# Value products with differences of two blocks' values, the sink column written a block ahead, and an attention layer whose order a model of the run decides

## The chip, the cores and the metric

The kernel runs on one core of a Trainium2 chip. The metric is the device time of one launch in microseconds (us), as the median of several runs.

## The reference, cut to what matters

Two residual layers, each behind an RMSNorm, then a last RMSNorm. The first is grouped-query attention with a sliding window and one learned sink for each head, the second a pooling mixer. S = 4096 tokens, D = 1024, 16 query heads over 4 key/value heads of 64, float32 throughout.

```python
def swa_with_sinks(q, k, v, sinks):            # blocks of 128 tokens
    kc, vc = band(k), band(v)                  # the block before and the block itself
    s = einsum('bnqhgd,bnkhd->bnhgqk', qb, kc) * (1.0 / sqrt(HEAD_DIM))
    diff = qi + BLOCK - kj
    in_band = (diff >= 0) & (diff < WINDOW)    # WINDOW = 128
    s = where(in_band & not_pad, s, -inf)
    m = maximum(max(s, axis=-1), sink)
    p = exp(s - m)
    p = p / (p.sum(-1) + exp(sink - m))
    return einsum('bnhgqk,bnkhd->bnqhgd', p, vc)

def attn_layer(h, w_in, sinks, w_out):
    q, k, v, z = split(h @ w_in)
    return (swa_with_sinks(q, k, v, sinks) * silu(z)) @ w_out

def pool_layer(h, w_in, w_mix, scale, w_out):
    u, z = split(h @ w_in)
    p = multiscale_pool(u)                     # windows 2, 4, 8, 16, one for each group
    m = einsum('bsgc,gcd->bsgd', p, w_mix).reshape(B, S, 1024) * scale
    return (m * silu(z)) @ w_out
```

## The kernel before

**Numbers.** TensorE multiplies in a rounded float32 (`fp32r`). Each operand is therefore split into a high half (a copy by ScalarE, ACT) and a low half (source minus high half, by VectorE, DVE), and each product is made three times: high by high, high by low, low by high (`split_sb`, L129; `PASSES`). Such a copy into `fp32r` is called CAST in the profile.

**Steps and units.** The attention layer goes through the tokens in 8 steps `s` of 512. A step consists of units of 256 output columns: `k`, four `q`, `v`, four `z` (the gate) and, for the step before, four `out`. A unit is 48 matmuls of 128x512 (L267), the `v` unit 96 of 128x256 (L277); step 0 has 10 units and the others 14. Unit weights arrive in two halves of 1 MB. In step 0 `w_load` fetches them, `w_split` splits them and writes the halves to DRAM (`wparts`). Later steps fetch them back by `w_again` (L156), into three buffers. All DMAs named here are issued on SyncE's queue (SP).

**Attention blocks.** Between the units' matmuls lie the 16 blocks of a step, one for each key head `j` and each 128 queries `b`; `2_2_3` means step 2, `j` 2, `b` 3, and "block 10" counts them from 0. Each block is two tiles of 64 queries, which see 192 keys. A block has three parts. `it_scores` (L368): ACT writes the negated sink beside the scores into the PSUM tile `s`, of which there is one buffer (L370); PE makes eight matmuls 128x192 (L375); DVE folds the first and the last 64 keys into the same 64 columns, since a query uses just one of each pair (L380), and takes the extreme (L384); ACT makes four exponentials with their sums (L387); DVE takes the reciprocal and GpSimd (POOL) multiplies (L390). `it_turn` (L393): PE transposes `P` into `pT`, a PSUM tile of two buffers shared with `po`; ACT copies it to the high half of `m1` (L404); DVE makes the low half (L405) and, in other rows, a part of `m2` (L410). In the folded rows a probability belongs either to the earlier or to the later key. POOL's `affine_select` therefore keeps in `m1` the later keys alone (`upto`, L417), and in `m2` the earlier keys alone (`after`, L414 and L419). `it_pv` (L422): six value products into `po`, for each tile two of `m1` with the block's own values (`vm` or `vn`, L432) and one of `m2` with the earlier values (`vp` or `vq`, L433); ACT and DVE bring the result into `o`.

**Values.** `ev_v` (L318) splits the `v` unit's result into the two half-partition parts of `vm`. `v_twice` sends them by DMA to the other 64 partitions of `vp` and `vq`, and `v_again` copies to `vn` on POOL and to `vp`, `vq` on ACT.

**The next layer's weights.** From step 2 on, `seven_load` and `seven` (L510) split the pooling layer's weights, and write them to DRAM, four pieces a step. Each piece becomes four or seven casts on ACT (`part_u`, `part_z`, `part_o`, L130), whose tiles take turns in two `sl` slots: a cast can start when the DMA of the cast two before it has landed. The weight of `u` is first multiplied with `w_mix` in step 0 (`prep_load`, `prep_mm`).

**What sets the order.** Nothing is in a written order. `at(t, fn, ...)` gives each piece a time in units, and the table `T` (L35) holds the offsets: `turn` units after a block's scores come its transposes, `pv` later its products. At the end the pieces are issued in order of time:

```python
for t, _, fn, args in sorted(events, key=lambda e: e[:2]):
    fn(*args)
```

The builder then orders each engine's queue with a list scheduler: it steps through a modelled run and takes the earliest issued instruction that is ready by its model. So the queues follow `T` only roughly, and any change in one engine's work can move instructions on the others.

Of the kernel before, what the change touches and what calls it, by code (L numbers as in the profile page):

```python
# [8 lines left out]
F32 = mybir.dt.float32  # L9
# [11 lines left out]
G = 512  # L21
# [5 lines left out]
NKV = 4  # L27
# [7 lines left out]
T = dict(sqA=2.5, sqAd=0.82, rsA=5.5, sqB=5.8, sqBd=0.5, rsB=7.95, tot=0.8, spr=0.3, xs=2.3, frs=5.3, fin=6.8, turn=0.9, pv=0.8, ws0=1.0, ws1=0.3, wr0=1.0, wr1=0.5, vt=0.25, vtd=0.5, k0=2.9, kd0=0.8, k1=6.1, kd1=0.8, k2=9.3, kd2=0.8, k3=12.5, kd3=0.8, wl0=2.0, wl1=1.2, res=1.55, xl=1.5, hc=0.01, a0=2.3, a1=4.6, a2=6.8, a3=9.3, ad=0.55, op=0.5, e0=2.9, e1=5.14, e2=7.38, e3=9.62, ed=0.56, pl=1.3, pm=0.5, pmd=0.5, aturn=0.9, apv=0.8, kt=0.2)  # L35
# [10 lines left out]
def f32(ap):  # L46
    return ap.bitcast(F32)
# [3 lines left out]
def trunk_kernel(ctx, tc, xt, xm, ng, w_a_in, sinks, w_a_out, wu_t, wmix, pscale, w_b_z, w_b_out, fg, out):  # L51
# [55 lines left out]

    vm = sp.tile([128, NB + 1, NKV, 128], F32R, tag="vm", name="vm")
    vn = sp.tile([128, NB, NKV, 128], F32R, tag="vn", name="vn")
    vp = sp.tile([128, NB + 1, NKV, 128], F32R, tag="vp", name="vp")  # L110
    vq = sp.tile([128, NB + 1, NKV, 128], F32R, tag="vq", name="vq")
    nc.vector.memset(kt[:, :, :, 0:128].bitcast(F32), 0.0)
    nc.vector.memset(vm[64:128, 0].bitcast(F32), 0.0)
    nc.vector.memset(vp[:, 0].bitcast(F32), 0.0)
    nc.vector.memset(vq[:, 0].bitcast(F32), 0.0)
# [202 lines left out]
    def ev_v(U, s):  # L318
        ps = acc.pop(U)
        if s > 0:  # L320
            for t in (vm[64:128], vp, vq):
                nc.gpsimd.tensor_scalar(t[:, 0], f32(t[:, NB]), 1.0, 1.0, op0=ALU.mult, op1=ALU.mult)
        ps = ps.rearrange("p a (b d) -> p (a b) d", d=64)
        for r in (0, 1):
            src = ps[64 * r:64 * r + 64]
            own = vm[64 * r:64 * r + 64, r:r + NB]
            v = own.rearrange("p b j d -> p (b j) d")
            nc.scalar.copy(v[:, :, 0:64], src)
            nc.vector.tensor_sub(v[:, :, 64:128], src, f32(v[:, :, 0:64]))

    def v_twice():
        upper, lower = f32(vm[0:64, 0:NB]), f32(vm[64:128, 1:NB + 1])
        nc.sync.dma_start(f32(vp[64:128, 1:]), upper)
        nc.sync.dma_start(f32(vq[0:64, 1:]), lower)

    def v_again(b):
        for r, before in ((0, vp), (1, vq)):
            rows = slice(64 * r, 64 * r + 64)
            src = f32(vm[rows, b + r])
            nc.gpsimd.tensor_scalar(vn[rows, b], src, 1.0, 1.0, op0=ALU.mult, op1=ALU.mult)  # L340
            nc.scalar.copy(before[rows, b + 1], src)
# [26 lines left out]
    def it_scores(s, j, b):  # L368
        ps = rpsum.tile([128, 4, 256], F32, tag="s", bufs=1, name=f"s{s}_{j}_{b}")
        nc.scalar.copy(view(ps, 1, [(512, 2), (447, 2)]), nsink[:, j].unsqueeze(2).to_broadcast([128, 2, 2]))  # L370
        for c in range(2):
# [13 lines left out]
        P = sp.tile([128, 4, 136], F32, tag="P", bufs=2, name=f"P{s}_{j}_{b}")  # L385
        for i in range(4):
            nc.scalar.activation(P[:, i, 0:129], view(ps, 1 + 512 * (i // 2) + 319 * (i % 2), [(1, 129)]), AF.Exp,  # L387
                                 bias=mx[:, i:i + 1], scale=-1.0, accum_out=sm[:, i:i + 1])
        nc.vector.reciprocal(sm, sm)  # L389
# [3 lines left out]
    def it_turn(s, j, b):  # L393
# [6 lines left out]

        m1 = sp.tile([128, 2, 4, 128], F32R, tag="m1", bufs=1, name=f"m1_{s}_{j}_{b}")
# [5 lines left out]
        mu = m1.rearrange("p l (c u) x -> p u l c x", c=2)  # L407
        for u in range(2):
            wr, other = slice(64 * u, 64 * u + 64), slice(64 - 64 * u, 128 - 64 * u)
            nc.vector.tensor_sub(m2[other, u], pu[wr, u], f32(mu[wr, u, 0]))  # L410
            after = dict(pattern=[[0, 4], [-1, 64]], base=-1, channel_multiplier=1)
            upto = dict(pattern=[[0, 4], [0, 2], [1, 64]], base=0, channel_multiplier=-1)
            src = f32(mu[wr, u, 0]).rearrange("p c (r q) -> p c r q", r=2)
            nc.gpsimd.affine_select(out=m2[wr, u].rearrange("p c (r q) -> p c r q", r=2), in_=src, compare_op=ALU.is_ge, fill=0.0,  # L414
                                    **{**after, "pattern": [[0, 2], [0, 2], [-1, 64]]})
            mv = mu[wr, u].rearrange("p l c (r q) -> p (l c) r q", r=2)
            nc.gpsimd.affine_select(out=mv, in_=f32(mv), compare_op=ALU.is_ge, fill=0.0, **upto)  # L417
            mv = m2[other, u].rearrange("p c (r q) -> p (c r) q", r=2)
            nc.gpsimd.affine_select(out=mv, in_=f32(mv), compare_op=ALU.is_ge, fill=0.0, **after)  # L419
        its[s, j, b] = (m1, m2)  # L420

    def it_pv(s, j, b):  # L422
        m1, m2 = its.pop((s, j, b))
        if b == 0:
            obufs[s, j] = sp.tile([128, 2, G], F32, tag="o", bufs=2, name=f"o{s}_{j}")
# [37 lines left out]
    def prep_load(g):  # L463
# [5 lines left out]
        split_sb(pw[g][:, 0], pw[g][:, 1], raw)  # L469
        for c in range(2):  # L470
# [3 lines left out]
            split_sb(t[:, 0], t[:, 1], raw)  # L474
# [360 lines left out]
    def unit(kind, s, j, t):  # L835
# [12 lines left out]
        elif s == 0:  # L848
# [3 lines left out]
            at(t - T["ws1"], w_split, u, 1, key)  # L852
# [40 lines left out]
    for g in range(1, 4):  # L893
        at(g - T["pl"], prep_load, g)
        for hf in range(2):
            at(g - T["pm"] + T["pmd"] * hf - 0.0005, prep_mm, g, hf)
# [237 lines left out]
```

## Time and profile before

| | us |
|---|---|
| median of 3 runs | 2742.24 |
| lowest and highest run | 2738.83, 2743.64 |
| the profiled execution's own time | 2741.26 |
| its span, first to last instruction | 2739.2 |
| attention layer, steps 0 to 7, about | 0 to 1700 |

A row of the profile's groups reads: line, engine, operation, output and inputs by the program's names (numbers left out; a name can stand for several tiles, `m` for `m1` and `m2`), shape and type, count; behind the first bar busy us and mean ns of one; behind the second the engine's idle time just before them and what released it. PE is TensorE's matmuls, PEld its weight loads. A row of the waits reads: what waited, for whom, us in total, times, longest. "x (n)" in a row of stretches is busy time and instructions. The granted clock is TensorE's, as a share of its full rate.

### The profile page before, as it was taken

Reading aid. Unit: us, or ns where it says so; the run is one execution under the profiler, and the core shown is the slowest. Engines: PE = TensorE matmul, PEld = TensorE weight load, DVE = VectorE, ACT = ScalarE, POOL = GpSimd, SP = SyncE. Lnnn points to the kernel's source line nnn. Section 1 sums busy time; section 2 is a strip of 40 time slices with the busy share of each in tenths; the row PEclk is TensorE's granted clock in tenths of the full one; section 3 lists DMA queues with packets and bytes.
Section 4 is the critical chain, followed back from the end, with each engine's and each line's share of the span. In section 5 each row is a group of like instructions: output and inputs, shape, how many; then the busy total and the mean of one; then the engine's idle time right before and its main releaser. Section 6 shows DMA issues by size and latency. Waiting matters only on the chain.

```text
span 2739.2 us, 35678 instructions
## 1 busy us (share of the span) xinstructions
PE 2602.2 (95%) x12604; PEld 2159.3 (79%) x12604; DVE 1626.7 (59%) x2546; ACT 1066.1 (39%) x2728; POOL 701.1 (26%) x1122
## 2 busy tenths in 40 slices
PE   7889998999998998999998999999999999999998
PEld 6778877877877886887887887788878887887786
DVE  6667666457456557556557556747455755655544
ACT  4556444445445445345444443313312331322121
POOL 0345443434334345335345333000000000000000
PEclk9999998999999999999999999999999999999999
DMA  7856766667667668667667555657577758757752
GB/s 285 278 200 226 264 215 221 226 223 251 230 211 272 231 200 250 232 215 267 225 200 257 191 200 210 237 192 263 175 242 256 263 195 288 267 186 244 255 200 100
DMA packets 175197, 626.10 MB, mean 229 GB/s; under 512 B 23198, under 2 KB 33438, under 8 KB 145324
## 3 DMA queue, kind: packets, MB, share of 16 engines
q1 hardware_dynamic: 175020, 623.83, 67.5%
q8 instruction: 100, 1.64, 0.2%
q14 instruction: 77, 0.63, 0.1%
HBM read 489.47 MB, written 117.51 MB: 222 GB/s over the span
## 4 chain that ended last, share of the span: by engine, by line
PE 50%; DVE 15%; DMA 14%; issue 13%; ACT 7%; POOL 1%; SPq 1%; ACTq 0%; POOLq 0%; DVEq 0%
PE mm L267 23%; DMA fin<-x 3%; PE mm L277 3%; PE s L375 2%; DMA out<-fin 2%; ACT P L387 2%; DMA w<-wparts 2%; DMA w_u<-part_u 2%; PE po L432 1%; DVE q L315 1%; PE pT L398 1%; DMA xm<-in_xm 1%; PE X_3u L620 1%; PE X_3z L620 1%; DVE m L410 1%
## 5 line engine op out<-in xcount | busy, mean ns | idle before, releaser
L267 PE MATMUL mm<-h,w 128*128 128x512 f32 x3456 | 871.2, 405 | 0.0
L267 PEld LDWEIGHTS mm<-h,w 128*128 128x128 f32 x3456 | 652.8, 194 | 140.9
L267 PE MATMUL mm<-a,w 128*128 128x512 f32 x1536 | 365.8, 393 | 4.2 <-DMA w<-wparts 2.4
L267 PEld LDWEIGHTS mm<-a,w 128*128 128x128 f32 x1536 | 284.2, 188 | 63.0 <-DMA w<-wparts 2.9
L390 POOL TENSOR_TENSOR P<-P,sm 128x516 f32<-128x516 f32 x128 | 135.5, 1059 | 463.4 <-DVE sm L389 459.1
L387 ACT ACTIVATE P<-s,mx 128x129 f32<-128x129 f32 x512 | 182.2, 370 | 140.9 <-DVE mx L384 138.2
L417 POOL TENSOR_SCALAR_AFFINE_SELECT m<-m 64x512 fp32r<-64x512 f32 x256 | 184.6, 721 | 54.3 <-DVE m L410 49.9
L747 POOL TENSOR_TENSOR rs<-ms,mhalf 128x4 f32<-128x4 f32 x7 | 7.0, 1007 | 742.1 <-DVE ms L746 742.1
L375 PEld LDWEIGHTS s<-kt,q 128*128 128x128 f32 x1024 | 135.2, 196 | 66.3 <-ACT s L370 52.1
L375 PE MATMUL s<-kt,q 128*128 128x192 f32 x1024 | 142.5, 281 | 43.2 <-ACT s L370 33.9
L414 POOL TENSOR_SCALAR_AFFINE_SELECT m<-m 64x256 fp32r<-64x256 f32 x256 | 109.9, 429 | 254.7 <-ACT m L404 246.0
L439 ACT COPY tmp<-po 64x256 f32<-64x256 f32 x256 | 94.1, 367 | 125.2 <-PE po L433 87.3
L440 DVE TENSOR_TENSOR o<-po,tmp 64x256 f32<-64x256 f32 x256 | 107.8, 421 | 45.9 <-ACT tmp L439 40.9
L315 DVE SCALAR_TENSOR_TENSOR q<-mm,q 64x512 fp32r<-64x512 f32 x128 | 88.1, 689 | 73.9 <-ACT q L314 72.6
L314 ACT ACTIVATE q<-mm 64x512 fp32r<-64x512 f32 x128 | 76.0, 593 | 138.0 <-DVE q L315 83.0
L419 POOL TENSOR_SCALAR_AFFINE_SELECT m<-m 64x256 fp32r<-64x256 f32 x256 | 123.5, 482 | 16.7
L410 DVE TENSOR_TENSOR m<-pT,m 64x256 fp32r<-64x256 f32 x256 | 108.2, 422 | 7.9
L405 DVE TENSOR_TENSOR m<-pT,m 128x512 fp32r<-128x512 f32 x128 | 88.0, 687 | 39.9 <-ACT m L404 38.9
L277 PE MATMUL mm<-w,h 128*128 128x256 f32 x768 | 100.6, 290 | 10.7 <-DMA w<-wparts 10.7
L277 PEld LDWEIGHTS mm<-w,h 128*128 128x128 f32 x768 | 97.9, 197 | 12.6 <-DMA w<-wparts 11.9
L380 DVE COPY_PREDICATED s<-mask,s 128x256 f32<-128x256 int8 x128 | 54.4, 425 | 89.8 <-PE s L375 79.0
L387 ACT ACTIVATION_READ_ACCUMULATOR P<-s,mx 128x1 f32 x512 | 104.5, 204 | 0.0
(356 smaller groups left out, 4545.5 us busy)
## 6 DMA issues: line engine op xcount, KB each, us to landing
w<-wparts SPq DMA_DIRECT2D x196, 1024.0 KB, 6.0
wparts<-w SPq DMA_DIRECT2D x28, 1024.0 KB, 4.8
xt<-in_xt SPq DMA_DIRECT2D x32, 512.0 KB, 4.5
res<-in_xt SPq DMA_DIRECT2D x32, 512.0 KB, 5.2
x<-res SPq DMA_DIRECT2D x32, 512.0 KB, 5.7
xr<-x SPq DMA_DIRECT2D x32, 512.0 KB, 6.1
xm<-in_xm SPq DMA_DIRECT2D x28, 512.0 KB, 6.0
w_u<-part_u SPq DMA_DIRECT2D x56, 256.0 KB, 3.5
```

Source lines behind the costliest of these rows:

```text
L267: nc.tensor.matmul(ps[:, c], w[:, wl, k % 4, 128 * c:128 * c + 128], rhs(k, hl), start=(k == 0 and i == 0), stop=(k == NK - 1 and i == 2))
L277: nc.tensor.matmul(ps[:, b], hts[s, k][:, hl, 128 * b:128 * b + 128], wtiles[U, k // 4][:, wl, k % 4], start=(k == 0 and i == 0), stop=(k ...
L315: nc.vector.scalar_tensor_tensor(dst[64 - r:128 - r], src, -SCALE, f32(dst[r:r + 64]), op0=ALU.mult, op1=ALU.subtract)
L375: nc.tensor.matmul(ps[:, 2 * c + u, 2 - 2 * u:194 - 2 * u], qs[s, j][:, c, 2 * b + u].rearrange("p r x -> p (r x)"), kt[:, j, hl, t:t + 19 ...
L387: nc.scalar.activation(P[:, i, 0:129], view(ps, 1 + 512 * (i // 2) + 319 * (i % 2), [(1, 129)]), AF.Exp, bias=mx[:, i:i + 1], scale=-1.0, ...
L390: nc.gpsimd.tensor_mul(P[:, :, 0:129], P[:, :, 0:129], sm.unsqueeze(2).to_broadcast([128, 4, 129]))
L410: nc.vector.tensor_sub(m2[other, u], pu[wr, u], f32(mu[wr, u, 0]))
L414: nc.gpsimd.affine_select(out=m2[wr, u].rearrange("p c (r q) -> p c r q", r=2), in_=src, compare_op=ALU.is_ge, fill=0.0, **{**after, "patt ...
L417: nc.gpsimd.affine_select(out=mv, in_=f32(mv), compare_op=ALU.is_ge, fill=0.0, **upto)
L419: nc.gpsimd.affine_select(out=mv, in_=f32(mv), compare_op=ALU.is_ge, fill=0.0, **after)
L439: nc.scalar.copy(tmp[d:d + 64], pv[e:e + 64, r])
L440: nc.vector.tensor_add(dst, pv[d:d + 64, r], tmp[d:d + 64])
```

## The change

**Values.** `ev_v` now keeps the whole result in float32 (`vf`, 128x1024), splits the block's own values for all 128 partitions (`vn`), then forms earlier values minus own values in PSUM, and splits these differences into `vp` (lower half of the partitions) and `vq` (upper half). `v_twice` sends those to the other halves, and `v_again` copies `vn` to `vm` on POOL alone. The products of `m1`, no longer masked, with the own values then count the folded rows as if all belonged to the later key, and those of `m2`, masked to the earlier keys, with the difference correct it. So the select `upto` is gone, 256 instructions on POOL; the matmuls are as many and of the same shapes.

**Sink.** The sink column of the following block is written right behind a block's exponentials (`s_open`, `opened`, `following`).

**Step 0.** The low half of every unit's second weight half, but for `out`, and of six of `prep_load`'s twelve pieces goes to POOL. The last two of the four `prep_load` come earlier.

**Spacing.** In `T`, the transposes and products follow the scores after .72 and .55 units instead of .9 and .8 (steps 1 to 6), the first product of a step comes no earlier than 4.5 units into it, and step 1 has its own order of units.

**Order.** All pieces of the attention layer's eight steps are issued in one block of the program, whose queues the builder orders by a finer model of the run's times; the rest follows as before.

```diff
     def ev_v(U, s):
...
+        src = ps.rearrange("p b (j d) -> p (b j) d", d=64)
+        nc.scalar.copy(vf[:, 1:], ps)
+        nc.scalar.copy(v[:, :, 0:64], src)
+        nc.vector.tensor_sub(v[:, :, 64:128], src, f32(v[:, :, 0:64]))
+        nc.vector.tensor_sub(ps, vf[:, 0:NB], ps)
+        for r, t in ((0, vp), (1, vq)):
+            rows = slice(64 * r, 64 * r + 64)
+            v = t.rearrange("p b j d -> p (b j) d")[rows]
+            nc.scalar.copy(v[:, :, 0:64], src[rows])
+            nc.vector.tensor_sub(v[:, :, 64:128], src[rows], f32(v[:, :, 0:64]))
...
         for i in range(4):
             nc.scalar.activation(P[:, i, 0:129], ...)
+        if (s, j, b) in following:
+            opened[following[s, j, b]] = s_open(*following[s, j, b])
...
-            mv = mu[wr, u].rearrange("p l c (r q) -> p (l c) r q", r=2)
-            nc.gpsimd.affine_select(out=mv, in_=f32(mv), compare_op=ALU.is_ge, fill=0.0, **upto)
...
             at(t - T["ws0"], w_split, u, 0, key)
-            at(t - T["ws1"], w_split, u, 1, key)
+            at(t - T["ws1"], w_split, u, 1, key, None if kind == "out" else nc.gpsimd)
...
-                at(t + turn + pv, it_pv, s, j, b)
+                at(max(t + turn + pv, base + T["pv0"]), it_pv, s, j, b)
...
-    for t, _, fn, args in sorted(events, key=lambda e: e[:2]):
+    early = [e for e in events if e[0] < base - A_OUT]
+    with tc.block(schedule_with_timeline_sim=True):
+        for _, _, fn, args in early:
+            fn(*args)
+    for _, _, fn, args in events[len(early):]:
         fn(*args)
```

How the queues move is shown at three places. A row is a line of the code, an operation, its output and inputs with their running numbers, the shape, and how often it stands there in a row.

ACT in step 2, from the exponentials (`P`) of block 2_2_2 to those of block 2_2_3, before: `m1` is the copy of the transposes, `tmp` that of the products, `s` the sink, `part_o` the casts.

```order
L387 ACTIVATE P2_2_2_5434,sm2_2_2_5432<-s2_2_2_5420,mx2_2_2_5431 128x129 x4
L439 COPY tmp2_2_0_5458<-po2_2_0_5451 64x256
L404 CAST m1_2_2_1_5477<-pT2_2_1_5472 128x512
L370 COPY s2_2_3_5556<-nsink_146 128x2x2
L130 CAST part_o0_0_1_6141<-raw7_o0_0_6060 128x256
L130 CAST part_o0_0_2_6145<-raw7_o0_0_6060 128x256
L130 CAST part_o0_0_3_6149<-raw7_o0_0_6060 128x256
L130 CAST part_o0_1_0_6567<-raw7_o0_1_6448 128x256
L387 ACTIVATE P2_2_3_5570,sm2_2_3_5568<-s2_2_3_5556,mx2_2_3_5567 128x129 x4
```

The same stretch after:

```order
L395 ACTIVATE P2_2_2_5367,sm2_2_2_5365<-s2_2_2_5270,mx2_2_2_5364 128x129 x4
L374 COPY s2_2_3_5372<-nsink_146 128x2x2
L445 COPY tmp2_2_0_5315<-po2_2_0_5308 64x256
L131 CAST part_o0_0_0_6030<-raw7_o0_0_5955 128x256
L315 ACTIVATE q2_3_5376<-mm34_5225 64x8x64
L131 CAST part_o0_0_1_6034<-raw7_o0_0_5955 128x256
L131 CAST part_o0_0_2_6038<-raw7_o0_0_5955 128x256
L445 COPY tmp2_2_1_5421<-po2_2_1_5414 64x256 x2
L415 CAST m1_2_2_2_5472<-pT2_2_2_5467 128x512
L131 CAST part_o0_0_3_6042<-raw7_o0_0_5955 128x256
L131 CAST part_o0_1_0_6451<-raw7_o0_1_6342 128x256
L395 ACTIVATE P2_2_3_5500,sm2_2_3_5498<-s2_2_3_5372,mx2_2_3_5497 128x129 x4
```

The sink has moved ahead of the copies, and the four casts in a row have become one and two pairs with other work between them.

PE in the same step, from the transposes (`pT`) of block 2_2_2 to its products (`po`), before; `mm` are the units' matmuls.

```order
L398 MATMUL pT2_2_2_5596<-ident_140,P2_2_2_5434 128x128 x4
L267 MATMUL mm35_5463<-h2_7_3972,w35_1_5396 128x512 x6
L267 MATMUL mm36_5626<-h2_0_3780,w36_0_5470 128x512 x6
L267 MATMUL mm36_5626<-h2_1_3791,w36_0_5470 128x512 x6
L267 MATMUL mm36_5626<-h2_2_3821,w36_0_5470 128x512 x6
L267 MATMUL mm36_5626<-h2_3_3867,w36_0_5470 128x512 x6
L267 MATMUL mm36_5626<-h2_4_3877,w36_1_5548 128x512 x6
L375 MATMUL s2_3_0_5666<-kt_160,q2_3_5441 128x192 x8
L432 MATMUL po2_2_2_5687<-m1_2_2_2_5601,vm_161 128x2x128 x2
L433 MATMUL po2_2_2_5687<-m2_2_2_2_5602,vp_163 128x2x128
L432 MATMUL po2_2_2_5687<-m1_2_2_2_5601,vn_162 128x2x128 x2
L433 MATMUL po2_2_2_5687<-m2_2_2_2_5602,vq_164 128x2x128
```

After:

```order
L408 MATMUL pT2_2_2_5467<-ident_140,P2_2_2_5367 128x128 x4
L383 MATMUL s2_2_3_5372<-kt_160,q2_2_4945 128x192 x6
L268 MATMUL mm35_5385<-h2_6_3902,w35_1_5303 128x512 x6
L268 MATMUL mm35_5385<-h2_7_3906,w35_1_5303 128x512 x6
L268 MATMUL mm36_5529<-h2_0_3734,w36_0_5392 128x512 x6
L268 MATMUL mm36_5529<-h2_1_3781,w36_0_5392 128x512 x6
L438 MATMUL po2_2_2_5549<-m1_2_2_2_5472,vm_161 128x2x128 x2
L268 MATMUL mm36_5529<-h2_2_3790,w36_0_5392 128x512 x2
L439 MATMUL po2_2_2_5549<-m2_2_2_2_5473,vp_163 128x2x128
L438 MATMUL po2_2_2_5549<-m1_2_2_2_5472,vn_162 128x2x128 x2
L439 MATMUL po2_2_2_5549<-m2_2_2_2_5473,vq_164 128x2x128
```

Twenty-four of the units' matmuls now stand between the transposes and the first products, where 36 stood.

SP at the start of step 3, before: `w40` is the weight of its `v` unit, `kt` the copy of the keys to the other partitions.

```order
L174 DMA xt4_0_7349<-in_xt 128x1024
L158 DMA w40_0_6054<-wparts_2_0_507 128x2048
L238 DMA rsq_4_116<-rs_4_6660 128x4
L304 DMA kt_160<-kt_160 64x2x512 x4
L158 DMA w40_1_6094<-wparts_2_1_593 128x2048
L242 DMA bc4_6664<-rsq_4_116 128x512
L174 DMA xt4_1_7426<-in_xt 128x1024
```

After, to the first weight of the unit behind it:

```order
L180 DMA xm4_3_6259<-in_xm 128x1024
L175 DMA xt4_0_7232<-in_xt 128x1024
L159 DMA w40_1_5997<-wparts_2_1_622 128x2048
L305 DMA kt_160<-kt_160 64x2x512 x4
L175 DMA xt4_1_7294<-in_xt 128x1024
L239 DMA rsq_4_116<-rs_4_6542 128x4
L159 DMA w41_0_6074<-wparts_14_0_2426 128x2048
```

The second half of the `v` unit's weight now stands ahead of the four copies of `kt`.

80 lines of the change are left out of this document (40 added, 40 removed).

## The prediction

> **What bounds the kernel now.** I read the page first, then the waits of TensorE (PE), then busy time in stretches cut at the same place of every step, then the timeline of ScalarE (ACT) where PE waits.
>
> ```profile
> span 2739.2 us, 35678 instructions
> PE 2602.2 (95%) x12604; PEld 2159.3 (79%) x12604; DVE 1626.7 (59%) x2546; ACT 1066.1 (39%) x2728; POOL 701.1 (26%) x1122
> ```
>
> PE is the bound, and the change leaves its matmuls as many and as large as they were. So only PE's idle time and its clock can give something. Stretches (length; busy time of PE, weight loads, DVE, ACT and POOL; granted clock; DMA share; GB/s): first the front of a step, then the tails, blocks 10 to 15, of steps 1 to 6.
>
> ```profile
> 262.00:382.00 120.00, 118.60 (x606) 99.57 (x604) 74.07 (x125) 60.63 (x175) 53.19 (x82) 1.00 0.73 250
> 382.00:478.00 96.00, 82.95 (x406) 69.86 (x407) 60.66 (x101) 41.55 (x114) 43.34 (x62) 0.88 0.64 214
> 598.00:685.00 87.00, 79.80 (x407) 66.41 (x408) 57.25 (x100) 40.90 (x112) 39.77 (x62) 0.94 0.71 240
> 806.00:894.00 88.00, 78.44 (x406) 65.73 (x406) 57.19 (x102) 40.81 (x114) 38.17 (x58) 0.94 0.75 258
> 1016.00:1107.00 91.00, 81.37 (x409) 68.33 (x407) 59.93 (x103) 40.98 (x113) 42.30 (x65) 0.91 0.76 238
> 1228.00:1311.00 83.00, 76.12 (x391) 62.82 (x390) 55.32 (x97) 39.92 (x110) 37.56 (x57) 0.96 0.73 250
> 1432.00:1517.00 85.00, 77.10 (x402) 65.15 (x403) 57.16 (x99) 37.84 (x110) 38.24 (x57) 0.94 0.68 220
> ```
>
> A front loses 1.4 us in 120, at full clock. The six tails hold 530 us, of which PE is busy 475.8: 54.2 us idle. Each length times one minus its clock adds up to 38.6 us. So about 93 us are to be had here. What PE waits for (us in total, times, longest):
>
> ```profile
> PE s L375 <- ACT s L370: 33.9, 22, 4.7
> PE po L432 <- POOL m L417: 14.8, 26, 1.5
> PE pT L398 <- DVE m L410: 12.8, 8, 4.2
> PE mm L277 <- DMA w<-wparts: 10.7, 6, 3.0
> PE po L433 <- POOL m L419: 3.9, 7, 1.0
> ```
>
> The largest is for the sink column, which ACT writes into the scores' PSUM tile. Why ACT is late shows in step 2's tail (start, duration):
>
> ```profile
> 597.75 0.71 ACT L130 CAST part_o<-raw_o 128x256 fp32r<-128x256 f32 x2
> 602.68 0.41 ACT L130 CAST part_o<-raw_o 128x256 fp32r<-128x256 f32 x1 [4.22 <-DMA wo<-part_o]
> 609.51 0.41 ACT L130 CAST part_o<-raw_o 128x256 fp32r<-128x256 f32 x1 [6.42 <-DMA wo<-part_o]
> 609.83 0.36 ACT L387 ACTIVATE P<-s,mx 128x129 f32<-128x129 f32 x1
> 611.35 0.37 ACT L439 COPY tmp<-po 64x256 f32<-64x256 f32 x1
> 612.23 0.17 ACT L370 COPY s<-nsink 128x4 f32<-128x4 f32 x1
> ```
>
> PE's timeline there:
>
> ```profile
> 612.45 1.14 PE L375 MATMUL s<-kt,q 128*128 128x192 f32 x8 [1.65 <-ACT s L370]
> ```
>
> Four casts of the next layer's weights stand in a row. They share two slots, so the third and fourth wait 4.22 and 6.42 us for writes to land. The softmax's exponentials stand behind them, and the sink for the next block stands behind a further two copies.
>
> **The change, part by part.** Idle time first.
>
> Sink written ahead. At 612.23 the sink comes 0.88 us after 611.35, where it now stands (right behind the exponentials): 0.88 of that wait of 1.65. Half or more of 33.9 us then goes; late exponentials keep the rest. I take -20, between 0 and -33.9.
>
> Fewer masks. POOL and the chain behind the transposes (busy, mean ns; idle and releaser):
>
> ```profile
> L417 POOL TENSOR_SCALAR_AFFINE_SELECT m<-m 64x512 fp32r<-64x512 f32 x256 | 184.6, 721 | 54.3 <-DVE m L410 49.9
> L419 POOL TENSOR_SCALAR_AFFINE_SELECT m<-m 64x256 fp32r<-64x256 f32 x256 | 123.5, 482 | 16.7
> L414 POOL TENSOR_SCALAR_AFFINE_SELECT m<-m 64x256 fp32r<-64x256 f32 x256 | 109.9, 429 | 254.7 <-ACT m L404 246.0
> L404 ACT CAST m<-pT 128x512 fp32r<-128x512 f32 x128 | 75.3, 588 | 59.5 <-PE po L432 46.8 <-PE po L433 7.7 <-PE pT L398 1.0
> ```
>
> A row of the chain of waits prices PE's matmuls, 0.231 us each:
>
> ```profile
> 339.66 8.32 PE mm L267 x36
> ```
>
> The removed select is 256 x 0.721 = 184.6 us of POOL, which is not the bound. What counts is the chain: POOL's share of a block falls from 2 x (0.429 + 0.721 + 0.482) = 3.26 us to 1.82, and the first two value products wait for ACT and DVE alone. Against that, PE's cover shrinks. For block 2_2_2 the old order has 36 projection matmuls (8.3 us) and 8 score matmuls between transposes and products; the new one has 24 (5.5 us) and 6. The cover loses about 3.1 us, the chain 1.4. I take 0: the gain of at most 18.7 us can turn into 26 waits longer by 1.7 us, +44.
>
> The casts. What ACT waits for in them:
>
> ```profile
> L130 ACT CAST part_z<-sum_z 128x256 fp32r<-128x256 f32 x32 | 13.0, 405 | 31.6 <-DMA w_z<-part_z 31.3
> L130 ACT CAST part_u<-sum_u 128x256 fp32r<-128x256 f32 x32 | 12.8, 405 | 36.4 <-DMA w_u<-part_u 36.0
> L130 ACT CAST part_o<-raw_o 128x256 fp32r<-128x256 f32 x32 | 12.6, 404 | 28.3 <-DMA wo<-part_o 26.9 <-DMA w_z<-part_z 1.1
> ```
>
> That is 94.2 us, and nothing in the change shortens a write. But the new order holds no run of more than two casts, where the old one had three runs of three and three of four; 92 stand alone instead of 65. More of ACT's own work hides the writes. By the order, with durations from the groups, the work between a cast and the second one after it grows from 3.2 us to 3.8 in the mean: at most 130 x 0.56 = 73 us less waiting on ACT. Little of that is on PE's path, which has 8 us of cover for a 10 us hold-up. I take -10, between 0 and -20.
>
> The value unit's weights. Their second half is issued ahead of the four copies of kt from step 3 on, no longer behind them: -6 of 10.7, between 0 and all.
>
> Step 0. The low halves of nine more weight tiles go from DVE to POOL:
>
> ```profile
> L131 POOL TENSOR_TENSOR w<-wraw,w 128x1024 fp32r<-128x1024 f32 x1 | 2.9, 2868 | 11.4 <-DMA xm<-in_xm 11.4
> L131 DVE TENSOR_TENSOR w<-wraw,w 128x1024 fp32r<-128x1024 f32 x27 | 34.3, 1271 | 11.7 <-ACT w L130 11.6
> ```
>
> DVE sheds 9 x 1.271 = 11.4 us, POOL gains 9 x 2.868 = 25.8, and probabilities queue behind each. The transposes' 12.8 us of waiting for DVE lie nearly all in this step. I take -4, between -12.8 and +6 (two POOL splits in the path).
>
> The clock. After a long wait PE runs at half rate:
>
> ```profile
> 1056.42 2.02 PE L375 MATMUL s<-kt,q 128*128 128x192 f32 x8 [4.68 <-ACT s L370]
> 1058.25 2.81 PE L267 MATMUL mm<-h,w 128*128 128x512 f32 x6
> ```
>
> Six matmuls in 2.81 us are 0.47 each, against 0.231 above. After the 1.65 us wait the eight score matmuls took 1.14, so short waits do not cost this. Of 38.6 us I take -18, about half, since the idle terms remove some 36 of the tails' 54 us, but not all of the long waits; between 0 and -38.6. [...]
>
> What is new:
>
> ```profile
> L328 ACT CAST vm<-mm 64x1024 fp32r<-64x1024 f32 x16 | 16.2, 1010 | 11.3 <-DVE vm L329 10.6 <-PE mm L277 0.6
> L329 DVE TENSOR_TENSOR vm<-mm,vm 64x1024 fp32r<-64x1024 f32 x16 | 19.6, 1222 | 1.5 <-ACT vm L328 1.1
> ```
>
> The copies of vq to the other partitions (view of that tile), and the page's row of instruction fetches:
>
> ```profile
> DMA to landing us min/median/max: 7.4/9.0/10.6
> ```
>
> ```profile
> q8 instruction: 100, 1.64, 0.2%
> ```
>
> The value eviction's chain grows from two copies and two subtractions (4.5 us) to about 2 x 1.01 + 2 x 1.222 + 1.01 + 2 x 1.222, some 8 us. The out unit behind it on PE (48 x 0.231 = 11.1 us) still covers the PSUM slot. Then the copy to the other half of the partitions has to land, up to 10.6 us later: 18.6 in all and about 1 us of issue and other work, where the order leaves 20.5 us of PE work before the first product. It fits by a hair: +2, between 0 and +14 (2 us in seven steps). The mid-steps' transposes follow the scores after some 9.5 us instead of 12.4; the way there (mask, maximum, exponentials, POOL) takes 4.2 to 6 us where ACT is free: +4, between 0 and +20. The block adds a branch to each queue: the 100 packets of instructions took 0.2% of 16 engines' span, 0.88 us each, so +2, between 0 and +4. [...]
>
> The sum: -20 + 0 - 10 - 6 - 4 - 18 + 2 + 4 + 2 = -50 on the profiled execution's 2741.3, so 2691; the median of the runs lies 1 us above it: 2692.
>
> **The rivals.** *The casts keep the tails.* The writes are no faster, and PE waits for late exponentials instead of the sink. Then half of the sink's wait, the weights and a little clock go (-17 - 6 - 5), the costs stay (+8): 2722. For it: 6.42 us of one wait stand ahead of the exponentials in either order if the write is that late. Against: the new order's shorter runs.
>
> *The shorter cover decides: slower.* In the tails ACT copies the transposes late, behind casts; PE now comes for the products 3.1 us sooner with a chain 1.4 us shorter. If all 36 tail blocks (six in each of six tails) fall short by that 1.7 us, it costs 61 us, and half of that again in clock, against the 50 gained: 2783. It decides from 1.4 us a block. Against: most waits for POOL were under 1 us, and the first products need no POOL now.
>
> *The tails become like the fronts.* All 93 us go, step 0 gives 4, the costs stay: 2652. For it: nothing in the tails but order holds PE back, with DVE busy 57 of 87 us. Against: the two slots.
>
> *The new order changes where PE waits, not how long:* 2742.
>
> **How the numbers follow.** Forecast (2660 to 2715) 0.55; casts keep the tails 0.15; shorter cover 0.15; tails like fronts 0.08; no change 0.07. The range 2645 to 2750 takes in all but the shorter cover and the outer ends of the terms. Within 0.2%, 5.5 us, is about what a measurement cannot tell from no change. Faster 0.55 + 0.15 + 0.08 = 0.78; within 0.06; slower 0.16.
>
> **What would show it.** Right: the wait of the scores for the sink under 15 us; none of the products for the removed select; tails with a clock above 0.96 and under 85 us; ACT's idle time ahead of the casts under 60 us. Wrong: products waiting for POOL's two selects or for ACT's copy by more than 20 us, fronts longer than 122 us, transposes waiting for POOL in step 0, or a gap of several us where the block ends.

## The result and the profile after

The changed kernel takes 2661.37 us in the median (2654.44 to 2664.78), the one before 2740.53: a ratio of 0.9713, 95% interval 0.9681 to 0.9745, so 79 us less. The head of the page after (span; busy time of each engine):

```profile
span 2657.1 us, 35166 instructions
PE 2560.8 (96%) x12604; PEld 2137.5 (80%) x12604; DVE 1623.5 (61%) x2545; ACT 1039.5 (39%) x2680; POOL 558.1 (21%) x875
```

To see where the time went I cut both spans where a step's value unit ends. From the second to the eighth of these ends lie six whole steps. Length, busy times, clock, DMA share and GB/s there, before and then after:

```profile
262.10:1517.60 1255.50, 1190.86 (x6063) 998.97 (x6062) 753.51 (x1319) 581.00 (x1699) 527.41 (x825) 0.97 0.69 231
```

```profile
263.60:1444.60 1181.00, 1152.29 (x6068) 973.74 (x6067) 762.70 (x1336) 565.50 (x1667) 395.67 (x628) 0.99 0.73 246
```

74.5 of the 82 us between the two spans are here. PE's idle time went from 64.6 us to 28.7, which is 35.9 us. The other 38.6 are busy time that as many matmuls no longer take. The time the clock withheld accounts for 32.5 of them: by the trace's clock records, without rounding, 39.3 us before (a mean clock of 0.9687) and 6.8 after (0.9942). Ahead of the stretch nothing was gained (262.1 and 263.6 us); behind it 9.1 us were (1221.6 and 1212.5), which I did not follow further.

The stretches of after that answer to those of the prediction: the front of step 1, then the six tails, cut at the scores of the same block. (That block, 2_2_3 in step 2, is number 11 counted from 0; the prediction called it 10. So a tail holds five blocks, and the six tails 30, not 36. The prediction's tail of step 5 starts 2.4 us behind its block's scores.)

```profile
263.70:378.40 114.70, 111.88 (x569) 94.30 (x568) 75.13 (x122) 56.13 (x158) 40.61 (x61) 0.99 0.74 251
378.40:466.50 88.10, 83.16 (x451) 68.76 (x450) 58.54 (x107) 44.72 (x126) 33.45 (x50) 1.00 0.79 253
586.10:661.00 74.90, 72.18 (x402) 61.18 (x401) 53.88 (x95) 40.39 (x111) 29.72 (x41) 1.00 0.84 284
779.50:856.80 77.30, 72.03 (x403) 60.99 (x402) 55.76 (x97) 41.36 (x114) 24.43 (x38) 1.00 0.87 293
975.90:1058.70 82.80, 76.57 (x408) 64.22 (x407) 60.31 (x103) 41.97 (x114) 32.30 (x45) 0.96 0.79 266
1177.20:1254.20 77.00, 73.06 (x402) 62.67 (x401) 54.71 (x97) 40.27 (x111) 29.77 (x41) 0.98 0.82 272
1372.70:1444.70 72.00, 71.30 (x402) 61.06 (x401) 53.61 (x96) 37.26 (x106) 22.10 (x36) 1.00 0.81 264
```

The tails of steps 2 to 6 take 72 to 83 us; before, they took 83 to 91. Step 1's cannot be compared by its length: its units have a new order, and the tail holds 451 matmuls where it held 406. In all six tails PE is idle 23.8 us; before, it was 54.2. What PE waits for now (us in total, times, longest):

```profile
PE mm L278 <- DMA w<-wparts: 8.1, 5, 2.7
PE pT L408 <- POOL P L400: 6.9, 14, 1.6
PE po L438 <- DVE m L423: 6.3, 3, 5.5
...
PE s L383 <- ACT s L374: 4.1, 6, 1.8
```

The wait for the sink fell from 33.9 us to 4.1, and those of the products for POOL (18.7) are gone. The matmuls of the value units stand idle as long as before, 10.7 us:

```profile
L278 PE MATMUL mm<-w,h 128*128 128x256 f32 x768 | 102.8, 291 | 10.7 <-DMA w<-wparts 8.1 <-issue 2.0 <-DVE kt L299 0.5
```

ACT, though, waits for the slots of its casts as before:

```profile
L131 ACT CAST part_z<-sum_z 128x256 fp32r<-128x256 f32 x32 | 13.0, 405 | 28.9 <-DMA w_z<-part_z 28.8
L131 ACT CAST part_u<-sum_u 128x256 fp32r<-128x256 f32 x32 | 13.0, 406 | 28.0 <-DMA w_u<-part_u 27.1 <-DVE sz L352 0.6
L131 ACT CAST part_o<-raw_o 128x256 fp32r<-128x256 f32 x32 | 12.6, 408 | 26.8 <-DMA wo<-part_o 24.5 <-DMA w_z<-part_z 1.4 <-ACT h L131 0.8
L131 ACT CAST part_u<-raw_u 128x256 fp32r<-128x256 f32 x16 | 6.4, 409 | 11.8 <-DMA w_u<-part_u 6.1 <-DMA wo<-part_o 5.6
L131 ACT CAST part_z<-raw_z 128x256 fp32r<-128x256 f32 x16 | 6.3, 411 | 6.0 <-DMA w_z<-part_z 3.6 <-DMA w_u<-part_u 2.3
```

Of before, the two last groups read:

```profile
L130 ACT CAST part_u<-raw_u 128x256 fp32r<-128x256 f32 x16 | 6.5, 405 | 4.5 <-DMA w_u<-part_u 4.0 <-DMA wo<-part_o 0.4
L130 ACT CAST part_z<-raw_z 128x256 fp32r<-128x256 f32 x16 | 6.3, 404 | 0.8 <-DMA w_u<-part_u 0.6
```

Idle time ahead of the five groups: 28.9 + 28.0 + 26.8 + 11.8 + 6.0 = 101.5 us after, and with the three rows of the prediction 31.6 + 36.4 + 28.3 + 4.5 + 0.8 = 101.6 before. ACT waits about as long as before, but PE hardly waits for ACT now. Block 2_2_3 shows how; first ACT's timeline (start, duration, what; idle time and its releaser in brackets), then PE's:

```profile
589.94 0.41 ACT L131 CAST part_o<-raw_o 128x256 fp32r<-128x256 f32 x1 [4.76 <-DMA wo<-part_o]
...
594.42 0.41 ACT L131 CAST part_o<-raw_o 128x256 fp32r<-128x256 f32 x1 [2.15 <-DMA wo<-part_o]
595.12 0.41 ACT L131 CAST part_o<-raw_o 128x256 fp32r<-128x256 f32 x1 [0.29 <-DMA wo<-part_o]
595.43 0.37 ACT L395 ACTIVATE P<-s,mx 128x129 f32<-128x129 f32 x1
```

```profile
586.66 0.89 PE L383 MATMUL s<-kt,q 128*128 128x192 f32 x6
...
598.40 0.66 PE L408 MATMUL pT<-ident,P 128*128 128x128 f32 x4 [0.28 <-POOL P L400]
```

The block's scores are done at 587.55, and its exponentials still come 8 us later, behind casts that waited 4.76 and 2.15 us. But PE has other work until 598, and its transposes wait 0.28 us. The block is no exception. In the 25 tail blocks of steps 2 to 6 the first exponential starts 7.0 us behind the end of the scores in the mean (before, 9.2), in the 55 other blocks of these steps 2.9 (before, 2.9).

### The profile page after: what moved, and what is told of

Same layout as the page of the kernel before. It is cut to its first block, busy times and chain, and to the rows that moved or that the text cites. A ratio compares the mean times of both kernels' runs of the same rounds, so it can differ in the third digit from the quotient of the medians.

```text
span 2657.1 us, 35166 instructions
## 1 busy us (share of the span) xinstructions
PE 2560.8 (96%) x12604; PEld 2137.5 (80%) x12604; DVE 1623.5 (61%) x2545; ACT 1039.5 (39%) x2680; POOL 558.1 (21%) x875
## 4 chain that ended last, share of the span: by engine, by line
PE 38%; issue 31%; DMA 15%; DVE 11%; ACT 4%; POOL 1%; SPq 0%; POOLq 0%; ACTq 0%; DVEq 0%
PE mm L268 23%; DMA w_u<-part_u 3%; PE mm L278 3%; PE s L383 2%; DMA w<-wparts 2%; DMA w_z<-part_z 2%; DMA xm<-in_xm 2%; DMA fin<-x 1%; PE po L438 1%; PE pT L408 1%; ACT P L395 1%; DVE h L132 1%; DVE sz L352 1%; DVE m L423 1%; PE X_3z L626 1%
## 5 line engine op out<-in xcount | busy, mean ns | idle before, releaser
L268 PE MATMUL mm<-h,w 128*128 128x512 f32 x3456 | 857.2, 398 | 9.4 <-DVE sz L352 3.8
L268 PEld LDWEIGHTS mm<-h,w 128*128 128x128 f32 x3456 | 636.4, 190 | 147.9 <-DVE sz L352 4.6
L268 PE MATMUL mm<-a,w 128*128 128x512 f32 x1536 | 372.4, 394 | 3.0 <-DMA w<-wparts 3.0
L383 PE MATMUL s<-kt,q 128*128 128x192 f32 x1024 | 148.1, 277 | 4.1 <-ACT s L374 4.1
L316 DVE SCALAR_TENSOR_TENSOR q<-mm,q 64x512 fp32r<-64x512 f32 x128 | 88.1, 688 | 71.6 <-ACT q L315 69.8
L278 PE MATMUL mm<-w,h 128*128 128x256 f32 x768 | 102.8, 291 | 10.7 <-DMA w<-wparts 8.1
L415 ACT CAST m<-pT 128x512 fp32r<-128x512 f32 x128 | 75.2, 587 | 69.1 <-PE pT L408 65.7
```

Source lines behind the costliest of these rows:

```text
L268: nc.tensor.matmul(ps[:, c], w[:, wl, k % 4, 128 * c:128 * c + 128], rhs(k, hl), start=(k == 0 and i == 0), stop=(k == NK - 1 and i == 2))
L278: nc.tensor.matmul(ps[:, b], hts[s, k][:, hl, 128 * b:128 * b + 128], wtiles[U, k // 4][:, wl, k % 4], start=(k == 0 and i == 0), stop=(k ...
L316: nc.vector.scalar_tensor_tensor(dst[64 - r:128 - r], src, -SCALE, f32(dst[r:r + 64]), op0=ALU.mult, op1=ALU.subtract)
L383: nc.tensor.matmul(ps[:, 2 * c + u, 2 - 2 * u:194 - 2 * u], qs[s, j][:, c, 2 * b + u].rearrange("p r x -> p (r x)"), kt[:, j, hl, t:t + 19 ...
```

## The experiments

Theory: the queues' order. The finer model places each block's parts so that the casts' hold-ups fall where PE has other work. Rivals: the sink written ahead, the fewer masks, the spacing. Each part was added to the kernel before or undone in the one after. "Six steps" is the stretch from the second to the eighth end of a value unit: its length and PE's idle time.

| kernel | median us | ratio to before, 95% | six steps us | idle us |
|---|---|---|---|---|
| after | 2661.37 | 0.9713 (0.9681 to 0.9745) | 1181.0 | 28.7 |
| b_block: before + block | 2707.91 | 0.9861 (0.9839 to 0.9882) | 1209.4 | 43.2 |
| b_sink: before + sink ahead | 2738.95 | 0.9984 (0.9972 to 0.9996) | 1241.6 | 58.3 |
| b_val: before + new values | 2731.29 | 0.9949 (0.9931 to 0.9968) | 1245.0 | 71.4 |
| a_noblock: after, no block | 2756.78 | 1.0047 (1.0030 to 1.0063) | 1279.5 | 97.2 |
| a_oldT: after, old spacing | 2692.27 | 0.9823 (0.9802 to 0.9845) | 1201.8 | 47.4 |
| a_noblock_oldT: both | 2726.30 | 0.9944 (0.9926 to 0.9962) | 1234.5 | 61.4 |
| a_nosink: after, sink late | 2660.09 | 0.9697 (0.9676 to 0.9718) | 1180.6 | 30.5 |
| a_mask: after, old values | 2692.16 | 0.9814 (0.9796 to 0.9833) | 1193.7 | 32.3 |
| a_turn: after, old distances | 2673.09 | 0.9758 (0.9733 to 0.9784) | 1195.7 | 41.1 |
| a_dve0: after, splits on DVE | 2649.87 | 0.9686 (0.9662 to 0.9709) | 1175.2 | 25.0 |
| b_direct: before, no casts | 2669.17 | 0.9760 (0.9734 to 0.9786) | 1188.8 | 31.4 |
| a_direct: after, no casts | 2660.44 | 0.9718 (0.9695 to 0.9741) | 1189.0 | 34.8 |

Below, a change in us is its ratio's distance from 1, times 2740; between rows not measured together it is uncertain by some 8 us, and by some 11 where one of the two is after.

**b_block.** The order alone, on the kernel before:

```diff
-    for t, _, fn, args in sorted(events, key=lambda e: e[:2]):
-        fn(*args)
+    with tc.block(schedule_with_timeline_sim=True):
+        for _, _, fn, args in early:
+            fn(*args)
```

> The kernel before, with one thing added: all pieces of the attention layer are issued in the block that the finer model orders. Values, masks, sink, table and step 0 are as before. By the theory that the order of the queues is what gained (the sink and the casts come at better places because the model sees how late they are), most of the 79 us comes with this alone: 2690 or less. By the theory that the sink written ahead carries it, the sink still stands behind the copies and waits: 2725 to 2745, with 25 us or more of waiting for the sink left. By the theory that the masks carry it: no change, 2735 to 2745.

38 us faster: half of the gain, less than the theory of the order asked. Its waits:

```profile
PE mm L277 <- DMA w<-wparts: 24.8, 6, 7.1
PE po L432 <- POOL m L417: 15.7, 21, 2.5
PE s L375 <- ACT s L370: 12.1, 5, 4.4
```

The sink's wait fell from 33.9 us to 12.1 with the sink issued where it was. A new one came: the value unit's weights, 10.7 us before, 24.8 now. The second value unit ends at 274.8 us instead of 262.1, so the block lost 13 us ahead of the six steps.

**b_sink.** The sink alone:

```diff
             nc.scalar.activation(P[:, i, 0:129], ...)
+        if (s, j, b) in following:
+            opened[following[s, j, b]] = s_open(*following[s, j, b])
```

> The kernel before, with the sink column of the following block written right behind the exponentials, and nothing else. By the theory of the sink: its 33.9 us of waiting fall under 10, and the clock that long waits cost comes back with it, some 25 of 38 us in steps 1 to 6: 2685 to 2700. By the theory that late exponentials behind casts are the cause, and the sink only the first to show it, the wait moves to the transposes or to the mask behind the scores: 2720 to 2740. By the theory of the order alone: within 10 us of 2740.

4 us faster. By its time this fits the second and the third expectation. The waits show where the rest went:

```profile
PE po L440 <- POOL m L425: 26.4, 30, 3.7
PE s L381 <- ACT s L372: 17.7, 13, 2.8
PE pT L406 <- DVE m L418: 16.2, 10, 4.0
...
PE po L441 <- POOL m L427: 4.7, 6, 0.9
```

The sink's wait lost 16 us, the products' waits for POOL rose from 18.7 to 31.1, the transposes' from 12.8 to 16.2. The sink was only the first thing that showed the lateness, as the second expectation had it, but most of the wait moved to the value products, which that expectation did not name.

**b_val.** The values alone (the new `ev_v`, `v_twice`, `v_again`, the tile `vf`, and):

```diff
-            nc.gpsimd.affine_select(out=mv, in_=f32(mv), compare_op=ALU.is_ge, fill=0.0, **upto)
```

> The kernel before, with the value products of the change (differences of two blocks' values, the one select gone, the P tile shorter) and its two times for the copies of the values; sink, spacing, step 0 and order as before. By the theory of the masks: the 18.7 us of products waiting for POOL go, and some clock with them: 2710 to 2722. By my prediction's step (cover and chain cancel) the gain here, with the old longer cover, is the full 18.7 at most and no loss. By the theories of sink and order: 2730 to 2742, since the sink's wait of 34 us stays.

14 us faster by the ratio, so within the 18.7 us of my prediction's step; the median of 2731 lies in the range of the sink and order theories as well, and the time does not decide between them. In its profile the sink's wait rose to 39.8 us and that of the value weights to 19.2.

**a_noblock.** The kernel after without the block:

```diff
-    with tc.block(schedule_with_timeline_sim=True):
-        for _, _, fn, args in early:
-            fn(*args)
+    for _, _, fn, args in early:
+        fn(*args)
```

> The kernel after, with the pieces of the attention layer issued without the block, so that the builder's coarser model orders the queues; all else as after. By the theory of the order: 2700 or more, with runs of three and four casts and waits for ACT back. By the theory that sink and masks carry it: 2660 to 2675. By a mixture each way: about 2680.

13 us slower than the kernel before, 92 slower than after. Its largest waits:

```profile
PE pT L408 <- POOL P L400: 62.4, 30, 4.6
PE po L439 <- POOL m L425: 19.0, 25, 3.4
```

Transposes wait for probabilities that are not there yet. Counted along PE's queue at the full clock's matmul times (0.23 us for one of 128x512), the coarse model puts 6.9 to 9.5 us of work between the scores and the transposes of a block in steps 1 to 6, wherever it lies; the finer one 6.4 to 15.2, the longest in a tail (the kernel before, with the old spacing, 10.6 to 13.9). The expected runs of three and four casts did not come back: there is no run above two here either, and yet this kernel is the slowest. So the runs are not what makes this kernel slow, nor is the sink's place (a_nosink, below). The exponentials are no later than after: in the 25 tail blocks 6.5 us behind the scores, where after has 7.0. But PE has 7.6 to 9.0 us of work there between scores and transposes, where after has 8.6 to 13.0, and the transposes of these blocks wait 32.2 us, after 4.5. So at this spacing the finer order gains by giving PE more work where the probabilities are late. What it gains at the old spacing is not narrowed down as far.

**a_oldT and a_noblock_oldT.** The old numbers of `T` (but `vt` and `vtd`), step 1's old order and the old places of `prep_load`; the second without the block as well.

```diff
-turn=0.72, pv=0.55, ... k0=3.1, kd0=0.78, ... pl=0.8, ... kt=0.6, ... pv0=4.5
+turn=0.9, pv=0.8, ... k0=2.9, kd0=0.8, ... pl=1.3, ... kt=0.2, ... pv0=-99.0
...
-        elif s == 1:
-            order = [("q", 0), ("k", 0), ("v", 0), ...
```

> The kernel after, with the spacing of before: the table's old numbers (but for the times of the copies of the values), the old order of step 1's units and the old places of prep_load. Block, values, sink and step 0's splits stay. If the parts add up, the three alone gave 34.5 (block), 3.5 (sink) and 11 (values), so 2740 less 49: about 2693, and the new spacing is worth the 30 us that are left. By the theory that the finer model's order is nearly all, whatever the table: 2661 to 2672. By the theory that the shorter distances are a loss which the block only mends: under 2655.

> As the run with the old spacing, and the block left out too, so that values, sink and step 0's splits of the change stand in the old order's model and table. By the sum of the parts: 2740 less 3.5 and 11, about 2725. If the 14 us by which the kernel without the block lost to the one before came from the new spacing alone, this one is 25 to 35 us faster than that one's 2757. If they came from the splits on POOL or the new values, it stays at 2745 or more, with transposes waiting for POOL's multiply.

2692 and 2726 us where the sums of the parts said 2693 and 2725. With the old spacing, block, values and sink do add up. The new spacing costs 30 us under the coarse model (2726 to 2757) and gains 31 under the finer one (2692 to 2661): by my reading it is good only for a builder that knows where it must not be kept, but no run set single distances. In a_oldT the largest wait is for the value weights, 34.0 us.

**a_nosink.**

```diff
-        if (s, j, b) in following:
-            opened[following[s, j, b]] = s_open(*following[s, j, b])
```

> The kernel after, with each sink column written where the block's scores begin, as before. In the kernel before with the block added, the waits for the sink were still 12 us. By the theory of the sink (masks and order aside, it must be early): 2680 to 2690, with 15 to 25 us of waiting for it. By the theory that the finer model places the sink well enough by itself: 2659 to 2667.

2660: no difference from after; its wait for the sink is 2.8 us. The finer model finds the sink's place by itself.

**a_mask.** The old `ev_v`, `v_twice`, `v_again` and masks in the kernel after:

```diff
+            nc.gpsimd.affine_select(out=mv, in_=f32(mv), compare_op=ALU.is_ge, fill=0.0, **upto)
```

> The kernel after, with the values and masks of before: three selects for each tile, products with the earlier values themselves. By the gain of the values alone in the old kernel (11 us): 2672. By the theory that the shorter way from transposes to products (24 matmuls instead of 36) needs the shorter chain: the first product waits for the removed select in most of the 96 blocks of steps 1 to 6 by 0.5 us or more, so 2710 or above. By my prediction's bound (18.7 us and the clock on top): 2690.

28 us slower than after. That is the number of my bound (2690), in part by luck, as the places show. Products wait for POOL again:

```profile
PE po L442 <- POOL m L427: 17.6, 20, 3.1
...
PE po L443 <- POOL m L429: 4.6, 12, 0.8
```

But the waits are 32 in number, not one in most of 96 blocks. Of the profiled spans' difference 13 us lie in the six steps, 13 ahead of them (the second value unit ends at 276.2, not 263.6) and 6 behind. Why the part ahead grows is open.

**a_turn.** Only the distances:

```diff
-turn=0.72, pv=0.55
+turn=0.9, pv=0.8
```

> The kernel after, with two numbers of the spacing as before: transposes 0.9 units behind the scores and products 0.8 behind those (now 0.72 and 0.55), in steps 1 to 6. The rest of the new spacing stays, and with it the order of SP, where the second half of the value unit's weights still goes ahead of all or most copies of the keys. The old spacing as a whole cost 31 us under the finer model, with 34 us of PE waiting for those weights. By the theory that the weights' place carries the spacing's gain: within 8 us of after, 2655 to 2669, with under 15 us of that wait. By the theory that the shorter distances carry it: 2678 or more, with that wait as small.

12 us slower, hardly more than the uncertainty, and between the two expectations. Neither theory holds as it was put, since the wait for the value weights is not small:

```profile
PE mm L278 <- DMA w<-wparts: 24.2, 6, 6.9
```

After, the idle time at the same matmuls is 10.7 us. This one wait has grown by as much as PE's idle time in the six steps (28.7 to 41.1 us), although the weights are issued ahead of the keys' copies in most steps. It need not be what costs the time: in a_nosink the same row of the waits reads 14.0 us, after 8.1, at no loss of time. Why longer distances make the weights late is open.

**a_dve0.**

```diff
-            at(t - T["ws1"], w_split, u, 1, key, None if kind == "out" else nc.gpsimd)
+            at(t - T["ws1"], w_split, u, 1, key)
```

(and the same in `prep_load`.)

> The kernel after, with all low halves of step 0's weights on DVE again, but for the first unit's. My prediction gave these splits 4 us of gain, between 12.8 and a loss of 6. After, the stretch to the end of the first value unit is 10 us longer than before, with PE's clock at 0.91. By the theory that POOL's slower splits (2.97 us against 1.29) are what is late there: 2650 to 2658. By my prediction: 2665 or so. If the earlier prep_load is what lengthens that stretch: within 3 us of 2661.

2650 us, the fastest kernel run, but its interval overlaps that of after, and its profiled span is only 2.1 us shorter; the second value unit ends at 265.9 us, no sooner than after's 263.6. So the splits on POOL gained nothing; that they cost 7 us is not shown. The late end of the first value unit (91.8 us, before 81.3) goes with the block: it lies at 88.8 to 93.5 us in all eight kernels that have the block, b_block (93.0) among them, which has neither these splits nor the earlier `prep_load`, and at 81.3 to 86.2 in the six without.

**b_direct and a_direct.** The casts left out, of before and of after, with DVE's low halves and POOL's sums that belong to them; SP writes the loaded weights as they are, so the pooling layer works with other weights.

```diff
     def seven(key, hf):
...
-            split_sb(t[:, 0], t[:, 1], m)
-            nc.sync.dma_start(wseven[key][i][:, hf], f32(t))
+            nc.sync.dma_start(wseven[key][i][:, hf], raw[:, i % 2:i % 2 + 2].rearrange("p k (c d) -> p k c d", c=2))
```

> The kernel before, with the casts of the next layer's weights left out: ACT's casts, DVE's low halves and POOL's sums of them are gone, and SP writes as many bytes straight from the loaded weights (the pooling layer then works with other weights). PE's order in the attention layer keeps its distances. By my prediction's reading, that ACT's casts behind slow writes make the tails lose what the fronts don't: the stretch from the second to the eighth value unit, 1255 us with 64.6 idle and 38 of clock, falls to 1185 or less, and the time to 2670 or less. By the theory that the old order places the blocks badly whatever ACT does: 2720 or more, with 40 us of idle time left there.

> The kernel after, with the casts of the next layer's weights left out in the same way (the pooling layer then works with other weights). This is the fourth cell: before with casts 2740, without 2669; after with casts 2661. By the theory that the new order gains because blocks and casts no longer stand in each other's way: little is left to take, since the stretch from the second to the eighth value unit has 28.7 us of idle and 12 of clock after; 2640 to 2658, and the gap between the kernels, 79 us with casts, shrinks to 10 to 30. By the theory that the new order gains beside the casts (shorter chain, better places) and they cost as much as ever: 2600 or less.

Before falls by 66 us, after by nothing that can be measured (0.9713 and 0.9718): a gap of 79 us with the casts becomes one of 9 to 12 without. The six steps of the two:

```profile
261.70:1450.50 1188.80, 1157.43 (x6062) 978.21 (x6062) 673.80 (x1180) 533.92 (x1559) 459.25 (x761) 0.99 0.72 245
```

```profile
262.50:1451.50 1189.00, 1154.18 (x6068) 981.65 (x6067) 696.90 (x1196) 523.13 (x1527) 333.78 (x564) 0.99 0.73 245
```

The same length, with old spacing, masks and sink in the one and new ones in the other. In b_direct the waits that stood for ACT's and POOL's lateness have shrunk, though neither the sink nor the select was touched:

```profile
PE s L375 <- ACT s L370: 9.8, 6, 3.7
PE po L432 <- POOL m L417: 5.8, 12, 1.8
```

(33.9 and 14.8 us before.) The exponentials of the 25 tail blocks come 3.8 us behind their scores, instead of 9.2. The edit has a price of its own, the weight loads. Here is b_direct, the value units in the second row:

```profile
PE mm L267 <- DMA w<-wparts: 17.9, 10, 4.4
PE mm L277 <- DMA w<-wparts: 2.4, 3, 1.0
```

Together that is 20.3 us; before, it was 2.4 + 10.7 = 13.1. So the casts cost the old order 66 us or somewhat more. In a_direct these waits grew from 12.9 to 23.5 us, so what the casts still cost the new order can be as much as the edit's price, some 10 us; only the balance is nothing. How much of the 66 us is ACT's waiting, and how much the work that DVE and POOL lost with the casts, these runs do not part.

## Why the prediction was right or wrong

The sign, the place (the tails of steps 1 to 6) and the cause (softmax work behind casts that wait for landing writes) were right. The forecast of 2692 is 31 us too high; the rival in which the tails become like the fronts, 2652 with a chance of 0.08, came closest.

The sum was -50 and the spans of the two profiles differ by -82. The idle terms of the six steps (-20 - 10 - 6, and +8 for what is new) made -28, and PE's idle time there fell by 35.9. The clock's -18 stands against 38.6 us less of busy time, 32.5 of it by the clock records, step 0's -4 against +1.5, and the 9.1 us behind the six steps had no term. So the clock was the most mis-sized. That the idle terms came out near is luck, for their parts were not as forecast:

- **The casts (-10): the step that failed.** It priced how far ACT's waits would shrink with shorter runs of casts. They did not shrink, 101.6 and 101.5 us. What changed is what stands behind a waiting cast: the exponentials of the tails come 7.0 us behind their scores instead of 9.2, and PE has other work for nearly all of that time. "Little of that is on PE's path" was wrong for before: without casts it is 66 us faster. After, leaving them out gains nothing on balance.
- **The sink (-20).** The wait fell by 29.8 us, as its bound allowed, but not by writing it ahead: a_nosink has the wait at 2.8 us too, and alone the step is worth 4 us. The timeline price of 0.88 us was that of a symptom.
- **Fewer masks (0).** Undoing them costs 28 us, beyond the 18.7 I gave as the most. Cover and chain did not cancel: with the new chain PE's shorter cover was enough (products wait 6.3 us for DVE, 2.2 for ACT), with the old one it was not. A bound from the waits of before left out what they cost in the new order, and ahead of the six steps.
- **The clock (-18).** By the clock records 32.5 us came back in the six steps. The reading under the term was wrong: half the clock followed shorter waits too (last section), the wait of 1.65 us that the prediction shows among them. So the clock could come back behind short waits as well: the six steps of before have sixteen stretches at half clock, those of after three.
- **The value weights (-6).** They stand as long as before, 10.7 us. The order on SP was no guide.
- **Step 0 (-4).** No gain: 262.1 and 263.6 us to the end of the second value unit, and 10.5 us more to the end of the first.
- **What is new (+2 +4 +2).** No product waits for the copied `vp` or `vq`, but with the old spacing and the coarse model one does, in step 0 (4.1 us in b_val, 6.0 in a_noblock_oldT): the new chain is as tight as the prediction had it. Transposes wait 6.9 us for POOL's probabilities. The block in itself cost 13 us ahead of the six steps on the kernel before, and 1 with the new spacing and values together (262.5 in a_noblock, 263.6 after); with the new spacing and the old values the stretch is long again (276.2 in a_mask). The +2 for the branches of the block is shown by no run: the page of after counts 100 packets of instructions, as before, and between the six steps and 1700 us, where the block ends, PE's longest wait is 2.04 us, for a DMA of the next layer's weights.

Of the signs I had named, ACT's idle time ahead of the casts under 60 us did not come true. The others did, but for two tails: step 1's of 88.1 us and step 4's with a clock of 0.96.

## What to carry to other kernels

An engine off the path that waits is harmless or costly by what is queued behind the wait: here casts with the same 101 us of ACT's waiting, and the work of DVE and POOL that hangs on them, cost 66 us in one order and on balance nothing measurable in another. So ask of each wait who stands behind it, and take the cause away in a run (here the casts) rather than the first wait that shows it. And a table of distances, a model that orders and an edit that shortens a chain are not priced one by one: the same spacing was worth -31 us under one model and +30 under the other.

## What the runs showed of the hardware

**Waits of 1.65 and 0.81 us were followed by half the clock.** This is the place in before where the prediction shows a wait of 1.65 us; 0.81 us more of waiting follow it. Below stand the wait, then the stretch behind it with the granted clock third from the end:

```profile
614.39 0.79 PE L432 MATMUL po<-m,vm 128*128 128x256 f32 x2 [0.81 <-POOL m L417]
```

```profile
614.00:621.00 7.00, 6.56 (x19) 5.44 (x20) 5.82 (x9) 3.25 (x7) 1.93 (x5) 0.51 0.80 274
```

The eight score matmuls right behind the wait of 1.65 us ran at full rate (1.14 us for all eight), which is what the prediction saw; the clock halved 0.5 us after them, and the 128x512 matmuls up to 620.9 started 0.43 us apart instead of 0.23. In the six steps of before, the clock records have sixteen such stretches of 3.4 or 6.8 us. In the 3.4 us ahead of each, as long as the shorter stretches, PE stood idle 1.05 to 2.66 us in all, and eleven of the sixteen have no single wait over 2.91 us there. After, three stretches are left, and no wait in the six steps is over 2.74 us. So the prediction's reading of this place, that short waits do not cost the clock, does not hold here. Not every short wait was followed by half the clock: one of 2.02 us in after, near 842, was followed by no such stretch.

**Loads beside writes.** With the same bytes written, but no casts between the writes, PE waits longer for weight loads: 20.3 us instead of 13.1 in all (b_direct against before), and in the kernel after 23.5 instead of 12.9:

```profile
PE mm L268 <- DMA w<-wparts: 12.5, 6, 4.3
PE mm L278 <- DMA w<-wparts: 11.0, 5, 4.2
```

After, these two rows read 4.8 and 8.1 us. I had not expected that pacing writes, which the two slots do, might protect the loads beside them; that it is the pacing was not tried by itself.
